# Queries and keys split once at full height and placed by DMA; the keys' low part kept once, its score product on 64 rows

## The chip, the cores and the metric

The kernel runs on one core of a Trainium2 chip. The metric is the device time of one execution in microseconds (us), less is better. The chip holds inputs and outputs in HBM, works in SBUF (128 partitions) and accumulates matrix products in PSUM. The engines are TensorE (PE in the profile; its weight loads are PEld), VectorE (DVE), ScalarE (ACT), GpSimd (POOL) and SyncE (SP), which here issues the DMAs.

## The reference, cut to what matters

One decoder layer over 1024 tokens of width 1024: a layer norm, then mixing, then a feed-forward part, then a gated embedding, each with a residual and a layer norm. The change is in the mixing, which has 8 attention heads of 64 features beside four pooling groups:

```
proj = x @ w_in[i]
q, k, v, u = jnp.split(proj, [ATTN_WIDTH, 2 * ATTN_WIDTH, 3 * ATTN_WIDTH], axis=-1)
...
z = jnp.einsum("bhqd,bhkd->bhqk", q_blk.astype(jnp.float32), kf) * scale
mask = k_pos[None, :] < q_pos[:, None]
log_not = jnp.where(mask, jax.nn.log_sigmoid(-z), 0.0)
suffix = lax.cumsum(log_not, axis=3, reverse=True) - log_not
weights = jnp.where(mask, jnp.exp(jax.nn.log_sigmoid(z) + suffix), 0.0)
return jnp.einsum("bhqk,bhkd->bhqd", weights, vf)
```

The attention is strictly causal, and instead of a softmax it breaks a stick: each weight is a sigmoid times the product of the complements that lie between.

## The kernel before, in words

All products are float32 made of parts: a number is split into a high part that TensorE's one-pass type (fp32r) holds, and the rest, the low part. `split` (L63) does it with a copy on ScalarE (L65) and a subtraction on VectorE (L66). A full product is three passes (`mm3`, L68 to L71): high by high, and the two mixed ones.

**Stages.** First the layer norm of all eight token blocks with the values' projection (to about 98 us). Then the attention stage (about 98 to 375 us). Then the output projection, the feed-forward part and the gate; the change doesn't touch these.

**The attention stage.** Work goes over tiles of one head and one block of 128 queries: four pairs of heads (`pr`), two heads in a pair (`j`), eight blocks (`t`), 64 tiles. `weigh` (L380) makes the scores of a tile against all keys up to its block, in chunks of 512 (`CH`): two products into one PSUM bank (L396, L397), two sigmoids on ScalarE (L398, L399), a reverse scan on VectorE (L400), a product on GpSimd (L403). `turn` transposes the weights (L126) and splits them; `gather` (every second tile, L429) multiplies them by the values.

TensorE's order is written out by hand: `weigh` runs three tiles (`AHEAD`) before `turn` and `gather`. Between them a stream called `fill` hands out steps of three products each: the projections of queries and keys of the pairs, then those of the pooling groups. `fill.until` makes sure that a pair's key chunk is projected before its first tile is weighed. The other engines' order, SP's too, is laid out by the framework's scheduler; semaphores and slots are assigned by it. Tiles come from tagged pools; tag `K` has 14 slots of 128x1024 float32.

**Queries and keys.** `proj_chunk` projects 128 columns, the two heads of a pair, for 512 tokens: head 0 comes out on partitions 0 to 63, head 1 on 64 to 127 (`rows[0]`, `rows[1]`). A head's 64 features are half of the array's 128 rows, so the kernel lays two parts of a query one over the other: in `qs[j]` the high part lies in the head's own half, the low part in the other. `kh[j]` holds the head's high keys in both halves. One product on 128 rows, `qs` by `kh` (L396), so gives high by high and low by high at once. The third part, high by low, is a second product on 128 rows: `kl[j]` holds the low keys in the head's own half and zeros, set by a memset (L268), in the other (L397).

`q_out` and `k_out` evacuate a chunk head by head: for each of the two heads a copy on 64 partitions (L259, L272) and a subtraction on 64 partitions (L260, L273). The low queries are written straight to the other half by VectorE; the high keys go to the other half by one DMA on SP's queue per head (L274).

Of the kernel before, what the change touches and what calls it, by code (L numbers as in the profile page):

```python
# [8 lines left out]
F32 = mybir.dt.float32  # L9
F32R = mybir.dt.float32r  # L10
AF = mybir.ActivationFunctionType
ALU = mybir.AluOpType
# [4 lines left out]
P = 128  # L17
S = 1024
# [3 lines left out]
CH = 512  # L22
# [12 lines left out]
def hymba_layer(ctx: ExitStack, tc: tile.TileContext, x, p, emb_g, emb_b, w_in, attn_g, w_pool,  # L35
                pool_scale, w_out, ln1_g, ln1_b, w_up, w_down, ln2_g, ln2_b, w_ple, w_gate,
                ln3_g, ln3_b, out):
    nc = tc.nc
    V, A, G, T = nc.vector, nc.scalar, nc.gpsimd, nc.tensor
    x, out, p = x[0], out[0], p[0, 0]  # L40
# [11 lines left out]
    def slot(tag, name, dt=F32):  # L52
        return sb.tile([P, 1024], dt, name=name, tag=tag, bufs=BUFS[tag])
# [5 lines left out]
    def bank(tag, name="bk"):  # L59
        return pspool.tile([P, CH], F32, name=name, tag=tag, bufs=2)  # L60


    def split(src, h, l, eng=None):  # L63

        A.copy(out=h, in_=src)  # L65
        (eng or V).tensor_tensor(out=l, in0=src, in1=h.bitcast(F32), op=ALU.subtract)  # L66
# [156 lines left out]
    rows = [slice(0, HD), slice(HD, P)]  # L223
# [10 lines left out]
    def proj_chunk(c0, c, evacuate):  # L234

        fetch(c0)
        wh, wl = loaded[c0]
        pq = bank("b0", "pq")
        for k in range(NK):
            mm3(pq, wh[:, k, :], wl[:, k, :], x_ap(xh, k, c), x_ap(xl, k, c),  # L240
                k == 0, k == NK - 1)
            if k == 1 and blocks.index(c0) + 1 < len(blocks):
                fetch(blocks[blocks.index(c0) + 1])
            if k == NK - 1:
                evacuate(slice(c * CH, (c + 1) * CH), pq)
            yield True

    def queries_keys(pr):

        t = {}

        def q_out(cs, pq):
            if "qs" not in t:
                t["qs"] = [slot("K", "qs", F32R) for _ in range(2)]
            for j in range(2):
                r, r2, qs = rows[j], rows[1 - j], t["qs"][j]
                A.copy(out=qs[r, cs], in_=pq[r])  # L259
                V.tensor_tensor(out=qs[r2, cs], in0=pq[r], in1=qs.bitcast(F32)[r, cs],  # L260
                                op=ALU.subtract)

        def k_out(cs, pq):
            if "kl" not in t:
                t["kl"] = [slot("K", "kl", F32R) for _ in range(2)]
                t["kh"] = [slot("K", "kh", F32R) for _ in range(2)]
                for j in range(2):
                    G.memset(t["kl"][j].bitcast(F32)[rows[1 - j], :], 0.0)  # L268
            for j in range(2):
                r, kh = rows[j], t["kh"][j]  # L270
                hf = kh.bitcast(F32)
                A.copy(out=kh[r, cs], in_=pq[r])  # L272
                V.tensor_tensor(out=t["kl"][j][r, cs], in0=pq[r], in1=hf[r, cs], op=ALU.subtract)  # L273
                nc.sync.dma_start(out=hf[rows[1 - j], cs], in_=hf[r, cs])  # L274

        for c in range(2):
            fill.add(proj_chunk(pr * P, c, q_out))
            fill.add(proj_chunk(512 + pr * P, c, k_out), (pr, c))
        return t

    def head_parts(t, j):
        return t["qs"][j], t["kh"][j], t["kl"][j]


    pspill = dram.tile([NT, P, D], F32, name="pspill")
# [30 lines left out]
    embedded = {}  # L316
    pw, pt = [], []
    heads = {pr: queries_keys(pr) for pr in range(4)}
    def leave0(i):
        load(xspill[i], xn[i])  # L320
# [48 lines left out]
    def head_values(pr, j):  # L369
        vs, h = slot("VS", "vs", F32R), 2 * pr + j  # L370
        load(vs.bitcast(F32).rearrange("p (t d) -> p t d", d=P),
             vspill[:, :, h * P:(h + 1) * P].rearrange("t p d -> p t d"))
        return vs.rearrange("p (t d) -> p t d", d=P)
# [6 lines left out]
    def weigh(k):  # L380

        if k.t == 0:
            k.vs = head_values(k.pr, k.j)
        else:
            k.vs = tiles[tiles.index(k) - 1].vs
        t, n = k.t, k.n
        qs, kh, kl = head_parts(heads[k.pr], k.j)
        if n <= CH:
            ra = slot("ra", "ra")
            rr, aa = ra[:, 0:CH], ra[:, CH:S]  # L390
        else:
            rr, aa = slot("ra", "rr"), slot("ra", "aa")
        for c in range(0, n, CH):
            e = min(n, c + CH)
            z = bank("b2", "z")[:, 0:e - c]
            T.matmul(z, lhsT=qs[:, t * P:(t + 1) * P], rhs=kh[:, c:e], start=True, stop=False)  # L396
            T.matmul(z, lhsT=qs[:, t * P:(t + 1) * P], rhs=kl[:, c:e], start=False, stop=True)  # L397
            A.activation(out=rr[:, c:e], in_=z, func=AF.Sigmoid, scale=-0.125)  # L398
            A.activation(out=aa[:, c:e], in_=z, func=AF.Sigmoid, scale=0.125)  # L399
        V.tensor_tensor_scan(out=rr[:, 0:n][:, ::-1], data0=rr[:, 0:n][:, ::-1],  # L400
                             data1=diag[:, S - n:S][:, ::-1], initial=0.0,
                             op0=ALU.mult, op1=ALU.add)
        G.tensor_tensor(out=aa[:, 0:n - 1], in0=aa[:, 0:n - 1], in1=rr[:, 1:n], op=ALU.mult)  # L403
        G.memset(aa[:, n - 1:n], 0.0)
        k.aa = aa
# [116 lines left out]
    with tc.manual_schedule(engines={mybir.EngineType.PE}):  # L522
        for n in range(-AHEAD, len(tiles)):
            if n >= 0:
                k = tiles[n]
                turn(k)
            if n + AHEAD < len(tiles):
                ahead = tiles[min(n + AHEAD + 1, len(tiles) - 1)]
                if ahead.j == 0 and ahead.t % 4 == 0:
                    fill.until((ahead.pr, ahead.t // 4))  # L530
                weigh(tiles[n + AHEAD])
            fill.rate = RATES[0] if n < 48 else RATES[1]
            if n < 0:
                fill.run(3)
            else:
                fill.share(k.n / P + 1.5)
                if k.t % 2:
                    gather(k)
                for f, *args in later.pop(n, ()):
                    f(*args)  # L540
                if k.j == 1 and k.t == NT - 1:
                    rms_square(k.pr)
                    later.setdefault(n + 2, []).append((rms_stats, k.pr))
                    later.setdefault(n + 8, []).append((rms_apply, k.pr, 0))
                    later.setdefault(n + 10, []).append((rms_apply, k.pr, 1))
        fill.run(4)
        rms_stats(3)
        fill.finish()
        rms_apply(3, 0)
        rms_apply(3, 1)  # L550
# [219 lines left out]
    for r0 in range(0, NT, 3):  # L770
# [4 lines left out]
        for n, k in enumerate(korder):  # L775
# [4 lines left out]
            for i in tiles:  # L780
                ts = slice(i * P, (i + 1) * P)
                for c in range(2):
                    cs = slice(c * CH, (c + 1) * CH)
# [17 lines left out]
        for i in tiles:  # L801
            for c in range(2):
                cs = slice(c * CH, (c + 1) * CH)
                V.scalar_tensor_tensor(out=xr[i][:, cs], in0=xr[i][:, cs], scalar=ALPHA,
                                       in1=acc[i, c], op0=ALU.mult, op1=ALU.add)
# [10 lines left out]
    with tc.manual_schedule(engines={ET.PE, ET.DVE, ET.Activation, ET.Pool}):  # L816

        stats = {}
        for i in (6, 7):
            for c in range(2):  # L820
                cs = slice(c * CH, (c + 1) * CH)
                V.scalar_tensor_tensor(out=xr[i][:, cs], in0=xr[i][:, cs], scalar=ALPHA,
                                       in1=acc[i, c], op0=ALU.mult, op1=ALU.add)
# [404 lines left out]
```

## Time and profile before

| what | value |
|---|---|
| median of 3 runs | 1255.14 us (1253.67 to 1256.07) |
| the profiled execution's own time | 1257.93 us |
| its span, from the first to the last instruction | 1256.2 us |
| mean granted clock of TensorE | 0.974 |
| PE, DVE, ACT, POOL busy | 1171.2, 942.5, 558.9, 523.4 us |

The profile is that of one execution. Busy times are sums over the whole span and over stages that have different limits. The ends of matmuls are modelled, and they overlap, so TensorE's busy time is not its time at its peak. A granted clock of 1 is 2.4 GHz.

### The profile page before, as it was taken

How to read it: one execution, taken by the hardware profiler on the slowest of the kernel's cores; microseconds unless marked ns; L12 is line 12 of the kernel's file. 1: busy time of each engine (PE TensorE's matmuls, PEld its weight loads, DVE VectorE, ACT ScalarE, POOL GpSimd, SP SyncE). 2: the span in 40 equal slices, each digit the busy share in tenths (PEclk: the TensorE clock that was granted, in tenths of full speed). 3: DMA queues.
4: the chain of work that ended last, by engine and by line, in shares of the span. 5: the costliest groups of instructions: out<-in, count | busy, mean ns of one | idle time of the engine just before them, and what ended most of it. 6: DMA issues, size and time to landing. Idle time of an engine off the chain costs nothing.

```text
span 1256.2 us, 15453 instructions
## 1 busy us (share of the span) xinstructions
PE 1171.2 (93%) x5496; PEld 965.3 (77%) x5496; DVE 942.5 (75%) x1177; ACT 558.9 (44%) x948; POOL 523.4 (42%) x360
## 2 busy tenths in 40 slices
PE   7999998899988998699899999999999999998997
PEld 5877777787877875488688888878888888886876
DVE  6745878686865779777577677778878888876998
ACT  4325756576654243445444545555432334421111
POOL 3212443354651353333434234247644556473432
PEclk9999999899998999899899999999999999998999
DMA  9824111121226364378777887899655665432121
GB/s 338 292 111 134 32 53 59 43 59 44 81 89 222 131 219 134 100 254 264 261 262 260 270 269 245 268 406 379 219 168 200 210 218 182 154 122 80 68 84 67
DMA packets 123580, 221.48 MB, mean 176 GB/s; under 512 B 9456, under 2 KB 64240, under 8 KB 123504
## 3 DMA queue, kind: packets, MB, share of 16 engines
q1 hardware_dynamic: 123504, 220.50, 51.8%
q8 instruction: 43, 0.70, 0.2%
q14 instruction: 33, 0.27, 0.1%
HBM read 148.12 MB, written 70.25 MB: 174 GB/s over the span
## 4 chain that ended last, share of the span: by engine, by line
PE 62%; DVE 15%; DMA 7%; issue 5%; POOL 5%; ACT 5%; SPq 1%; DVEq 0%; POOLq 0%; ACTq 0%
PE pd L69 7%; PE pd L70 7%; PE pd L71 7%; PE pu L71 5%; PE pu L70 5%; PE pu L69 5%; PE pq L69 3%; PE tp L126 3%; PE pq L70 2%; PE pq L71 2%; PE o L429 2%; DVE rr L400 2%; POOL rs L103 2%; DVE xres L113 2%; DMA tspill<-draw 1%
## 5 line engine op out<-in xcount | busy, mean ns | idle before, releaser
L574 POOL TENSOR_TENSOR draw<-draw 128x512 f32<-128x512 f32 x64 | 101.8, 1590 | 185.6 <-DMA draw<-in_w_down_dram 183.0
L922 DVE TENSOR_TENSOR xres<-xres,pd 128x512 f32<-128x512 f32 x208 | 137.1, 681 | 46.8 <-PE pd L71 46.2
L574 POOL TENSOR_TENSOR dop<-draw,dop 128x1024 fp32r<-128x1024 f32 (+1 forms) x48 | 112.8, 2369 | 125.8 <-ACT dop L899 112.3
L899 ACT CAST dop<-draw 128x1024 fp32r<-128x1024 f32 (+1 forms) x96 | 81.0, 906 | 137.9 <-PE pd L71 51.1
L69 PE MATMUL pd<-dop 128*128 128x512 f32 x320 | 125.4, 392 | 0.9 <-DVE xres L922 0.8
L70 PE MATMUL pd<-dop 128*128 128x512 f32 x320 | 125.1, 391 | 1.0 <-POOL dop L574 1.0
L71 PE MATMUL pd<-dop 128*128 128x512 f32 x320 | 124.8, 390 | 0.0
L574 DVE TENSOR_TENSOR dop<-draw,dop 128x1024 fp32r<-128x1024 f32 (+1 forms) x48 | 84.2, 1754 | 4.4 <-ACT dop L899 4.4
L103 POOL TENSOR_TENSOR rs<-var,mhalf 128x1 f32<-128x1 f32 x32 | 44.0, 1376 | 104.4 <-DVE var L101 104.3
L740 ACT COPY hid<-pu 128x512 f32<-128x512 f32 x48 | 28.2, 588 | 125.1 <-PE pu L71 74.5
L69 PE MATMUL pq<-xh,wh 128*128 128x512 f32 x192 | 78.4, 408 | 0.8 <-DVE ul L66 0.8
L400 DVE TENSOR_TENSOR_SCAN rr<-rr,diag 128x640 f32<-128x640 f32 (+3 forms) x32 | 70.6, 2205 | 10.7 <-ACT rr L398 10.3
L403 POOL TENSOR_TENSOR aa<-aa,rr 128x639 f32<-128x639 f32 (+3 forms) x32 | 57.8, 1806 | 48.6 <-DVE rr L400 48.6
L71 PE MATMUL pq<-xh,wl 128*128 128x512 f32 x192 | 77.1, 401 | 0.0
L70 PE MATMUL pq<-xl,wh 128*128 128x512 f32 x192 | 76.8, 400 | 0.0
L69 PEld LDWEIGHTS pd<-dop 128*128 128x128 f32 x320 | 60.3, 189 | 14.6 <-DVE xres L922 1.2
L70 PEld LDWEIGHTS pd<-dop 128*128 128x128 f32 x320 | 60.3, 189 | 14.0 <-POOL dop L574 1.7
L71 PEld LDWEIGHTS pd<-dop 128*128 128x128 f32 x320 | 60.3, 189 | 12.5
L574 DVE TENSOR_TENSOR hid<-pu,hid 128x512 f32<-128x512 f32 x48 | 33.0, 688 | 44.4 <-PE pu L71 37.7
L66 DVE TENSOR_TENSOR atl<-tp,ath 128x512 fp32r<-128x512 f32 (+2 forms) x96 | 50.9, 547 | 17.4 <-ACT ath L65 16.7
L65 ACT CAST wh<-wraw 128x1024 fp32r<-128x1024 f32 x36 | 38.0, 1056 | 47.1 <-PE acc L70 25.4
L70 PE MATMUL acc<-wl,mix 128*128 128x512 f32 x128 | 51.7, 404 | 4.6 <-POOL wl L66 4.2
(241 smaller groups left out, 3360.7 us busy)
## 6 DMA issues: line engine op xcount, KB each, us to landing
hspill<-hid SPq DMA_DIRECT2D x48, 512.0 KB, 5.2
draw<-hspill SPq DMA_DIRECT2D x48, 512.0 KB, 6.1
uraw<-in_w_up_dram SPq DMA_DIRECT2D x32, 512.0 KB, 5.8
draw<-in_w_down_dram SPq DMA_DIRECT2D x32, 512.0 KB, 4.7
tspill<-draw SPq DMA_DIRECT2D x64, 256.0 KB, 4.4
wraw<-in_w_out_dram SPq DMA_DIRECT2D x24, 512.0 KB, 3.6
draw<-in_w_down_dram SPq DMA_DIRECT2D x48, 256.0 KB, 5.2
wraw<-in_w_in_dram SPq DMA_DIRECT2D x16, 512.0 KB, 4.7
```

What stands on the lines that cost most here:

```text
L65: A.copy(out=h, in_=src)
L66: (eng or V).tensor_tensor(out=l, in0=src, in1=h.bitcast(F32), op=ALU.subtract)
L69: T.matmul(ps, lhsT=lh, rhs=rh, start=start, stop=False, **kw)
L70: T.matmul(ps, lhsT=lh, rhs=rl, start=False, stop=False, **kw)
L71: T.matmul(ps, lhsT=ll, rhs=rh, start=False, stop=stop, **kw)
L103: G.tensor_tensor(out=rs, in0=var, in1=mhalf[:, 0:1], op=ALU.pow)
L126: T.transpose(tp[:, j * P:(j + 1) * P], src[:, (k0 + j) * P:(k0 + j + 1) * P], ident)
L400: V.tensor_tensor_scan(out=rr[:, 0:n][:, ::-1], data0=rr[:, 0:n][:, ::-1], data1=diag[:, S - n:S][:, ::-1], initial=0.0, op0=ALU.mult, op1 ...
L403: G.tensor_tensor(out=aa[:, 0:n - 1], in0=aa[:, 0:n - 1], in1=rr[:, 1:n], op=ALU.mult)
L574: eng.tensor_tensor(out=o, in0=i0, in1=i1, op=op)
L899: A.copy(out=h, in_=raw)
L922: V.tensor_tensor(out=xres[i][:, cs], in0=xres[i][:, cs], in1=src, op=ALU.add)
```

## The change

`q_out` splits a chunk for both heads at once, on 128 partitions, into a staging slot (`qp`); four DMAs then place the parts in `qs`, two for each head. `k_out` does the same: the high part goes into a staging slot (`kp`), and four DMAs place each head's high keys in both halves of its `kh`; the low part goes straight into one tile `kl` for both heads, each in its own half. No half of `kl` is zeroed. The second score product reads only the head's own 64 rows of `qs` and `kl`.

```diff
         t = {}
+
+        def place(dst, src, j):
+            nc.sync.dma_start(out=dst, in_=src[rows[j]])
 
         def q_out(cs, pq):
             if "qs" not in t:
                 t["qs"] = [slot("K", "qs", F32R) for _ in range(2)]
+            both = slot("K", "qp", F32R)
+            h, l = both[:, 0:CH], both[:, CH:S]
+            split(pq, h, l)
             for j in range(2):
-                r, r2, qs = rows[j], rows[1 - j], t["qs"][j]
-                A.copy(out=qs[r, cs], in_=pq[r])
-                V.tensor_tensor(out=qs[r2, cs], in0=pq[r], in1=qs.bitcast(F32)[r, cs],
-                                op=ALU.subtract)
+                qs = t["qs"][j].bitcast(F32)
+                place(qs[rows[j], cs], h.bitcast(F32), j)
+                place(qs[rows[1 - j], cs], l.bitcast(F32), j)
 
         def k_out(cs, pq):
             if "kl" not in t:
-                t["kl"] = [slot("K", "kl", F32R) for _ in range(2)]
+                t["kl"] = slot("K", "kl", F32R)
                 t["kh"] = [slot("K", "kh", F32R) for _ in range(2)]
-                for j in range(2):
-                    G.memset(t["kl"][j].bitcast(F32)[rows[1 - j], :], 0.0)
+            h = slot("K", "kp", F32R)[:, 0:CH]
+            split(pq, h, t["kl"][:, cs])
             for j in range(2):
-                r, kh = rows[j], t["kh"][j]
-                hf = kh.bitcast(F32)
-                A.copy(out=kh[r, cs], in_=pq[r])
-                V.tensor_tensor(out=t["kl"][j][r, cs], in0=pq[r], in1=hf[r, cs], op=ALU.subtract)
-                nc.sync.dma_start(out=hf[rows[1 - j], cs], in_=hf[r, cs])
+                kh = t["kh"][j].bitcast(F32)
+                for r in rows:
+                    place(kh[r, cs], h.bitcast(F32), j)
...
     def head_parts(t, j):
-        return t["qs"][j], t["kh"][j], t["kl"][j]
+        return t["qs"][j], t["kh"][j], t["kl"]
...
             T.matmul(z, lhsT=qs[:, t * P:(t + 1) * P], rhs=kh[:, c:e], start=True, stop=False)
-            T.matmul(z, lhsT=qs[:, t * P:(t + 1) * P], rhs=kl[:, c:e], start=False, stop=True)
+            r = rows[k.j]
+            T.matmul(z, lhsT=qs[r, t * P:(t + 1) * P], rhs=kl[r, c:e], start=False, stop=True)
```

## Rows read from the trace of the kernel before

**Rows 1.** The page's engine totals: busy us, share of the span, instructions.
```profile
PE 1171.2 (93%) x5496; PEld 965.3 (77%) x5496; DVE 942.5 (75%) x1177; ACT 558.9 (44%) x948; POOL 523.4 (42%) x360
```

**Rows 2.** Windows view of the attention stage, 100 to 375 us.
```profile
core 0: us, PE busy (x) PEld busy (x) DVE busy (x) ACT busy (x) POOL busy (x), PEclk, DMA share, GB/s
100.00:375.00 275.00, 254.25 (x1420) 216.08 (x1418) 206.80 (x258) 171.49 (x393) 128.18 (x149) 0.96 0.22 63
```

**Rows 3.** Chain of waits, 98 to 380 us: shares, then pieces (start, us).
```profile
by line: PE pq L69 10.2%; PE pq L70 9.8%; PE pq L71 9.7%; PE o L429 9.4%; PE tp L126 8.0%; DVE rr L400 8.0%; issue 6.6%; DVE atl L66 3.9%; PE z L396 3.7%; PE z L397 3.3%; ACT rr L398 3.0%; DVE wl L66 2.9%; ACT aa L399 2.6%; PE pm L447 2.3%;
...
113.23 2.25 DMA kh<-kh
...
131.17 0.68 DVE qs L260
...
287.52 0.60 DVE kl L273
```

**Rows 4.** Groups by line, 0 to 560 us: count, busy us, mean ns, idle before.
```profile
L396 PE MATMUL z<-kh,qs 128*128 128x512 f32 (+2 forms) x96 | 40.1, 418 | 6.1 <-ACT ra L399 3.9 <-DMA kh<-kh 2.1
L397 PE MATMUL z<-kl,qs 128*128 128x512 f32 (+2 forms) x96 | 33.8, 356 | 0.0
L260 DVE TENSOR_TENSOR qs<-pq,qs 64x512 fp32r<-64x512 f32 x16 | 11.0, 689 | 7.6 <-ACT qs L259 7.3
L273 DVE TENSOR_TENSOR kl<-pq,kh 64x512 fp32r<-64x512 f32 x16 | 10.9, 684 | 2.1 <-ACT kh L272 1.9
L259 ACT CAST qs<-pq 64x512 fp32r<-64x512 f32 x16 | 9.3, 583 | 13.1 <-PE pq L71 6.6 <-DVE qs L260 6.5
L272 ACT CAST kh<-pq 64x512 fp32r<-64x512 f32 x16 | 9.3, 582 | 7.0 <-DVE kl L273 6.5 <-PE pq L71 0.3
L268 POOL MEMSET kl<- 64x1024 f32 x8 | 7.6, 948 | 22.4 <-PE pe L70 22.0
L66 DVE TENSOR_TENSOR ul<-pq,uh 128x512 fp32r<-128x512 f32 x8 | 5.4, 678 | 3.0 <-ACT uh L65 3.0
L65 ACT CAST uh<-pq 128x512 fp32r<-128x512 f32 x8 | 4.8, 602 | 4.0 <-PE pq L71 4.0
```

**Rows 5.** Source view of L274: issue time on SP in ns, and landing.
```profile
L274 SPq DMA_DIRECT2D kh<-kh x16: 461/467/523, 94.0 to 288.8; - x16
...
DMA to landing us min/median/max: 2.2/2.3/3.7
```

**Rows 6.** Timeline of SP, 165 to 172 us, and two copies on ScalarE.
```profile
166.99 0.47 SPq L274 DMA_DIRECT2D kh<-kh  x1
167.77 0.37 SPq L74 DMA_DIRECT2D wraw<-in_w_in_dram  x1
169.31 0.47 SPq L274 DMA_DIRECT2D kh<-kh  x1
171.52 0.37 SPq L74 DMA_DIRECT2D vs<-vspill  x1
...
166.39 0.57 ACT L272 CAST kh<-pq 64x512 fp32r<-64x512 f32 x1
...
256.33 0.58 ACT L272 CAST kh<-pq 64x512 fp32r<-64x512 f32 x1 [0.30 <-PE pq L71]
```

**Rows 7.** Timeline of TensorE: first score products on those two key chunks.
```profile
172.75 0.48 PE L396 MATMUL z<-kh,qs 128*128 128x512 f32 x1
...
284.31 0.30 PE L396 MATMUL z<-kh,qs 128*128 128x128 f32 x1
```

**Rows 8.** Timeline of TensorE, 112.2 to 113.3 us: start, us.
```profile
112.25 0.39 PE L396 MATMUL z<-kh,qs 128*128 128x512 f32 x1
112.48 0.39 PE L397 MATMUL z<-kl,qs 128*128 128x512 f32 x1
112.71 0.38 PE L126 MATMUL tp<-ident,ra 128*128 128x128 f32 x2
112.84 0.48 PE L396 MATMUL z<-kh,qs 128*128 128x512 f32 x1
```

**Rows 9.** Timeline of weight loads, from 115.58 us, under products in flight.
```profile
115.69 0.19 PEld L397 LDWEIGHTS z<-kl,qs 128*128 128x128 f32 x1
115.80 0.19 PEld L69 LDWEIGHTS pq<-xh,wh 128*128 128x128 f32 x1
```

**Rows 10.** Windows view, 240 to 250 us; columns as in rows 2.
```profile
240.00:250.00 10.00, 10.00 (x41) 9.02 (x40) 4.29 (x4) 3.22 (x8) 4.82 (x5) 0.52 0.00 1
```

## The prediction

> **What bounds the kernel now.** I read the page's engine totals first, to see which engine could be the limit at all: TensorE is busy 93% of the span and VectorE 75% [rows 1]. That is an average over stages, and the change touches one of them, the attention stage. So I asked for that stretch alone, 100 to 375 us: TensorE 254.25 of 275 us, VectorE 206.80, ScalarE 171.49, GpSimd 128.18, DMA share 0.22 [rows 2]. The reader is to see that TensorE is nearest to full, that VectorE is not free either, and that the DMA engines have room.
>
> Next the chain of waits over the stretch, since a busy share doesn't say who waits for whom. TensorE holds 10.2 + 9.8 + 9.7 + 9.4 + 8.0 + 3.7 + 3.3 + 2.3 = 56.4% of it by the lines named, VectorE's scan 8.0%, its low parts (L66) 3.9% [rows 3]. So the stage is a weave: more than half of the time the end is set by TensorE's stream, the rest by short steps on VectorE and ScalarE that TensorE then waits for. The instructions that the change rewrites stand on this chain themselves: 14 pieces on L259, L260 and L273, from 131.17 to 287.52 us, sum 9.08 us; and one transfer of a key half, 2.25 us [rows 3].
>
> **The split, removed and added.** Each pair of heads has two chunks, so there are 8 query and 8 key evacuations. Before, each takes two copies and two subtractions on 64 partitions: 16 + 16 copies of 0.58 us, 9.3 + 9.3 us on ScalarE; 16 + 16 subtractions of 0.69 us, 11.0 + 10.9 us on VectorE [rows 4]. After, each takes one copy and one subtraction on 128 partitions. The pool's values go through just that pair already: 0.602 and 0.678 us at 128x512 [rows 4]; height costs nothing. So ScalarE sheds 18.6 - 16 x 0.60 = 9.0 us and VectorE 21.9 - 16 x 0.68 = 11.0 us. GpSimd sheds 8 memsets, 7.6 us [rows 4]; it is under half busy in the stage [rows 2], so I take nothing for it.
>
> Of this only what stands on the chain moves the end. Copy, subtraction, copy, subtraction run one behind the other (ScalarE sat idle 6.5 us before L259 and 6.5 us before L272 until the subtraction had ended [rows 4]); half of that series is left. Half of 9.08 is **-4.5 us**. Bounds: nothing, if other work on VectorE fills the place, and -11.0 us, if all that VectorE sheds came off the end.
>
> **The moves.** After, a query chunk and a key chunk are placed by four DMAs each: 64 in all where there were 16. An issue on SP takes 0.467 us, and one lands 2.3 us after it [rows 5]. SP thus gets 48 x 0.467 = 22.4 us more in a queue that carried one or two DMAs in ten microseconds here (between 165 and 172 us: four issues [rows 6]). Behind a move that waits for its copy or its subtraction stand, on SP, the next weight block and the next head's values, and ScalarE's weight cast waits for the former. Latency: before, copy, then one DMA: 0.58 + 2.3 us. After, the first head's key chunk needs two: 0.60 + 0.47 + 2.3, the last of four 0.60 + 3 x 0.467 + 2.3 = 4.3 us. What covers it is the lead of the projection: the copy for pair 1's second chunk is at 166.39 and its first score product at 172.75, 6.4 us [rows 6, 7]; pair 3's first chunk is copied at 256.33 and used at 284.31 [rows 6, 7]. Only the transfer at 113.23 had no cover [rows 3]; it ends one issue later, **+0.5 us** (bounds 0 and 1.4, all four). The query parts are projected a whole key chunk (24 products of some 0.23 us, 5.5 us) earlier. Of the 14 slots the long-lived tiles of a pair take 5 instead of 6; two short-lived staging slots come in. Nothing for either.
>
> **The second product on 64 rows.** Its streamed columns are unchanged, so by itself it costs what it did; nothing gained, since the next product needs all rows. But all 96 pairs of score products now alternate in height: into 64 rows and out again, 192 changes. No row shows a product of that height: the array part reads 128*128 everywhere, L396 and L397 included [rows 4]. What rows do show is how much equal heights overlap. Products of 512 columns start at 112.25 and 112.48, 0.23 apart, and each lasts 0.39 [rows 8]: 0.16 us of each runs under the next. The next weights also load under the product in flight, 0.11 apart [rows 9]. Lower bound of a change: 0, overlap as before. Upper bound: the product ends, then the weights load, 0.16 + 0.11 = 0.27 us. I take 0.16, an estimate: the product in flight is let run to its end before the other height starts, while the weights are fetched ahead as now; it lies between the ends, and uses only an overlap that rows show to exist. That makes 192 x 0.16 = 30.7 us of TensorE. TensorE holds 56.4% of the chain, and a delay counts where it does: **+17.3 us**. Bounds for that share: 27% (the score products' own 7.0% of 282 us is 19.7 us of their 40.1 + 33.8), 8.2 us; and all of it, 30.7 us.
>
> The Trainium skill, TensorEngine Tiling (Array Packing), section Tiling Modes, Key Properties, says that changing the tiling mode, as against the tile, drains the engine; no run here shows it yet. It gives no time; by it the sum is the one above, and without it the first rival's. The Trainium skill, TensorE: Matmul & The Clock Gate, Part 3, says that a weight load overlaps a product in flight only when their row groups differ. Here the measurement differs: [rows 9] has loads 0.11 us apart beneath products on the same 128 rows. By the page the load would wait in the forecast too, which is the second rival's sum.
>
> **The sum.** -4.5 + 0.5 + 17.3 = +13.3 us. It stands against the profiled execution: 1257.93 us, 1.73 beyond its span of 1256.2. The median of the runs shown is 2.79 lower, 1255.14; so the time forecast is 1255.1 + 13.3 = **1268.4 us**. Its own range, by the two shares: +4.2 to +26.7, 1259 to 1282.
>
> **Rivals.** *Height is free*: products of both heights follow each other 0.23 us apart. Then -4.5 + 0.5 = -4.0, 1251.1 us; at best -11, 1244. For it: kinds of TensorE work change without a gap now, transposes into score products at 112.71 and 112.84 [rows 8]. Against it: those all use the full array. It decides if a change costs under 4.0 / (192 x 0.564) = 0.037 us. *Weights wait too*: 0.27 us, 51.8 us of TensorE, x 0.564 = 29.2; less 4.0, +25.2, 1280 us; more if TensorE then holds the whole chain (+47.8, 1303). Against it: loads run ahead today [rows 9]. *The moves gate*: heights free, but SP's order puts a move behind a wait, and one place without cover pays a full 3 x 0.467 + 2.3 = 3.7 us: -4.0 + 3.7 = -0.3, 1254.8 us. For it: the 2.25 us on the chain and 4 times the DMAs [rows 3, 5]. Against: leads of 6 to 28 us, and SP nearly empty [rows 6, 7].
>
> **Chances.** Forecast 0.50: the change of height is the one new thing on the engine that is nearest to full, and a quarter of the price taken is enough to outweigh the gain. Height free 0.27; weights wait too 0.12; moves gate 0.11. About 0.2% is what a measurement of this kernel can tell from no change, 2.5 us. Faster: most of the first rival and a little of the last, 0.27. Within 0.2%: most of the last rival, the edge of the others, 0.10. Slower: forecast and second rival, 0.63. The range, 1247 to 1290, leaves out the best end of the free case and the worst of the third, under 2 in 10.
>
> **What the changed profile would show.** Right: L397's successors (and L397 itself) start some 0.39 us after the product before them instead of 0.23, with the array part 64*128; the stretch of attention longer by 10 to 20 us, all others unchanged; 16 copies and 16 subtractions at 128x512, 64 moves on SP, and the copy-subtraction pieces on the chain halved. Wrong: starts still 0.23 apart (first rival), loads that begin only at the product's end (second), TensorE waiting for moves (third). The forecast is wrong above all if the change of height is cheap, or if the copies' time on the chain was worth more than half; and if the gaps let the granted clock fall, as between 240 and 250 us (0.52) [rows 10], it is too low.

## The result, and the profile after

The changed kernel takes 1274.25 us (median of 4 runs, 1271.42 to 1280.91), against 1254.41 for the kernel before beside it: a ratio of 1.0157, 95% interval 1.0132 to 1.0182, some 19.7 us more. It is slower, as forecast; the forecast was 13.3 us more.

The execution profiled is the slowest of the four (1280.91 us), at a mean granted clock of 0.966 where the others had 0.971 to 0.976; its totals stand a little high for that. Its page's engine totals, to be held against [rows 1]:

```profile
PE 1210.9 (95%) x5496; PEld 975.1 (76%) x5496; DVE 922.1 (72%) x1161; ACT 552.7 (43%) x932; POOL 507.8 (40%) x352
```

VectorE and ScalarE have 16 instructions less each and GpSimd 8, as the split promised; TensorE is busy 39.7 us more with the same number of products, a part of it by the lower clock. Two of the four groups of the new split, at 128x512, against [rows 4]:

```profile
L65 ACT CAST qp<-pq 128x512 fp32r<-128x512 f32 x8 | 4.7, 592 | 9.3 <-PE pq L71 9.3
...
L66 DVE TENSOR_TENSOR kl<-pq,kp 128x512 fp32r<-128x512 f32 x8 | 5.5, 682 | 4.1 <-ACT kp L65 4.1
```

With their counterparts that is 11.0 us of VectorE where it was 21.9, and 9.4 of ScalarE where it was 18.6. The attention stage in the windows view, columns as in [rows 2], and the chain of waits from 98 to 400 us, against [rows 3]:

```profile
100.00:375.00 275.00, 269.16 (x1295) 205.46 (x1294) 178.15 (x221) 154.97 (x353) 106.40 (x136) 0.93 0.29 76
```

```profile
by line: PE pq L69 16.9%; PE pq L70 13.0%; PE pq L71 12.9%; PE o L434 11.9%; PE z L402 11.5%; PE tp L126 10.4%; PE z L400 7.9%; DMA qs<-qp 1.9%; PE pm L452 1.9%; DVE rr L405 1.4%; DVE atl L66 1.0%; issue 0.9%; POOL aa L408 0.9%; PE pb L465 
...
111.64 5.79 DMA qs<-qp
```

Three things are to be seen. TensorE is now full in the stage (269.16 of 275 us) and got through 1295 products in it instead of 1420. It holds 86.4% of the chain by the lines named, where it held 56.4%; VectorE's scan fell from 8.0% to 1.4%. And a new wait stands on the chain: 5.79 us for query moves, where 2.25 us was for a key half.

Now the products themselves. The timeline of TensorE and of its weight loads around one pair of score products, against [rows 8, 9]:

```profile
114.28 0.39 PE L71 MATMUL pq<-xh,wl 128*128 128x512 f32 x1
114.50 0.39 PE L400 MATMUL z<-kh,qs 128*128 128x512 f32 x1
114.82 0.50 PE L402 MATMUL z<-kl,qs 64*128 64x512 f32 x1
115.25 0.44 PE L126 MATMUL tp<-ident,ra 128*128 128x128 f32 x2
117.47 0.76 PE L400 MATMUL z<-kh,qs 128*128 128x512 f32 x1 [1.78 <-DMA qs<-qp]
```

```profile
114.28 0.19 PEld L400 LDWEIGHTS z<-kh,qs 128*128 128x128 f32 x1
114.82 0.18 PEld L402 LDWEIGHTS z<-kl,qs 64*128 64x128 f32 x1 [0.35 <-issue]
115.25 0.20 PEld L126 LDWEIGHTS tp<-ident,ra 128*128 128x128 f32 x2 [0.24 <-issue]
```

L400 follows L71 at the old distance. L402, on 64 of 128 rows, doesn't: its weight load, which used to begin 0.00 to 0.11 us behind the start of the product before it, begins 0.32 us behind, when that product is all but over (it ends at 114.89). Its own end comes 115.32 - 114.89 = 0.43 us after the last one's, where the same pair was 0.23 us apart in [rows 8]. The 0.32 is the shortest of its kind; the median of 41 such pairs of 512 columns at full clock is 0.41. What stays the same is the end: in all 83 changes into 64 rows at full clock, whatever the columns, the load begins 0.07 us before the modelled end of the product before it (at 512 columns it was 0.40 us before it in the kernel before). The way back costs as much: behind L402, whatever its columns, a product of 512 columns ended 0.43 us later (median of 70 cases; before, 0.24). So a change of height costs 0.20 us at 512 columns, 0.19 at 256 and 384, 0.14 at 128: about the length of the load itself (0.18 us in the row above), which is no longer hidden. Weighted by the counts of L402's forms (48, 16, 16, 16) that is 17.9 us into the low products and some 19 us out of them: about 37 us of TensorE for 192 changes.

The moves, last. First SP's timeline before the wait; then, by the tile view, the landing of the values' loads (104 to 107 us), of the moves of high parts (109.5 to 111.5 us), and of all query moves, against [rows 5]; then three windows, columns as in [rows 2]:

```profile
104.99 2.21 SPq L74 DMA_DIRECT2D vs<-vspill  x3
109.83 1.11 SPq L256 DMA_DIRECT2D qs<-qp  x2
111.04 0.53 SPq L74 DMA_DIRECT2D wraw<-in_w_in_dram  x1
111.64 2.50 SPq L256 DMA_DIRECT2D qs<-qp  x2
```

```profile
DMA to landing us min/median/max: 4.0/5.8/7.5
...
DMA to landing us min/median/max: 4.7/4.7/4.8
...
DMA to landing us min/median/max: 2.2/2.4/5.8
```

```profile
110.00:113.00 3.00, 3.00 (x15) 2.44 (x14) 1.81 (x3) 0.15 (x1) 0.00 (x0) 1.00 1.13 261
113.00:116.00 3.00, 2.69 (x12) 1.62 (x10) 1.12 (x1) 2.12 (x4) 0.00 (x0) 1.00 1.10 235
119.00:122.00 3.00, 3.00 (x8) 2.28 (x9) 1.49 (x1) 1.41 (x4) 0.26 (x3) 0.50 0.61 178
```

The two moves of high parts went out, then a 512 KB weight block, then the moves of low parts. Most moves land in 2.4 us; these took 4.2 to 5.8, while the DMA engines were full (share 1.13 and 1.10; a packet counts whole where it starts, so a share can pass 1). The weight block is not alone in this: the high parts went out ahead of it and took 4.7 us too, while two of three 512 KB loads of values, issued from 104.99 us on, were still landing. TensorE stood for 1.78 us, and ran at half clock behind it (0.50 from 119 to 122 us).

### The profile page after: what moved, and what is told of

It reads as the page before. It is cut to its first block, busy times and chain, and to the rows that moved or that the text cites. A ratio compares the mean times of both kernels' runs of the same rounds, so it can differ in the third digit from the quotient of the medians.

```text
span 1279.1 us, 15507 instructions
## 1 busy us (share of the span) xinstructions
PE 1210.9 (95%) x5496; PEld 975.1 (76%) x5496; DVE 922.1 (72%) x1161; ACT 552.7 (43%) x932; POOL 507.8 (40%) x352
## 4 chain that ended last, share of the span: by engine, by line
PE 73%; DVE 10%; DMA 6%; POOL 5%; issue 4%; ACT 2%; SPq 0%; DVEq 0%; POOLq 0%; ACTq 0%
PE pd L69 7%; PE pd L70 7%; PE pd L71 7%; PE pu L69 7%; PE pu L71 7%; PE pu L70 7%; PE pq L69 4%; PE pq L70 3%; PE pq L71 3%; PE tp L126 3%; PE o L434 3%; PE z L402 3%; PE z L400 2%; POOL rs L103 2%; DVE xres L113 2%
## 5 line engine op out<-in xcount | busy, mean ns | idle before, releaser
L71 PE MATMUL pd<-dop 128*128 128x512 f32 x320 | 125.0, 391 | 0.0
L69 PE MATMUL pq<-xh,wh 128*128 128x512 f32 x192 | 85.7, 447 | 1.6 <-DVE vst L66 1.6
L405 DVE TENSOR_TENSOR_SCAN rr<-rr,diag 128x640 f32<-128x640 f32 (+3 forms) x32 | 65.5, 2047 | 23.2 <-ACT rr L403 20.8
L71 PE MATMUL pq<-xh,wl 128*128 128x512 f32 x192 | 78.4, 408 | 0.0
L71 PEld LDWEIGHTS pd<-dop 128*128 128x128 f32 x320 | 60.5, 189 | 12.6
```

Of the source, the lines that this page charges most:

```text
L69: T.matmul(ps, lhsT=lh, rhs=rh, start=start, stop=False, **kw)
L71: T.matmul(ps, lhsT=ll, rhs=rh, start=False, stop=stop, **kw)
```

## The experiments

Two theories after the result. The first: the changes of height are the cost, and TensorE as the new bound eats what the split saves. The rival: the 48 added moves are the cost. All ratios are to the kernel before, run beside the experiment; a ratio of 1.001 is 1.25 us.

**One part alone, and the other.** In the first run the kernel before gets the 64-row product and nothing else; in the second the changed kernel gets its 128-row product back, with the low keys in two tiles with zeroed halves.

```diff
# e1_rows64_only, from the kernel before
-            T.matmul(z, lhsT=qs[:, t * P:(t + 1) * P], rhs=kl[:, c:e], start=False, stop=True)
+            r = rows[k.j]
+            T.matmul(z, lhsT=qs[r, t * P:(t + 1) * P], rhs=kl[r, c:e], start=False, stop=True)
# e3_rows128_moves, from the changed kernel
-                t["kl"] = slot("K", "kl", F32R)
+                t["kl"] = [slot("K", "kl", F32R) for _ in range(2)]
...
+                for j in range(2):
+                    G.memset(t["kl"][j].bitcast(F32)[rows[1 - j], :], 0.0)
             h = slot("K", "kp", F32R)[:, 0:CH]
-            split(pq, h, t["kl"][:, cs])
+            A.copy(out=h, in_=pq)
+            for j in range(2):
+                r = rows[j]
+                V.tensor_tensor(out=t["kl"][j][r, cs], in0=pq[r], in1=h.bitcast(F32)[r],
+                                op=ALU.subtract)
...
-            r = rows[k.j]
-            T.matmul(z, lhsT=qs[r, t * P:(t + 1) * P], rhs=kl[r, c:e], start=False, stop=True)
+            T.matmul(z, lhsT=qs[:, t * P:(t + 1) * P], rhs=kl[:, c:e], start=False, stop=True)
```

> The kernel before with one edit: the second score product reads only the head's own 64 rows; the split, the zeroed halves and the moves stay as before. If changes of height on TensorE are the cost (theory), all of it is here and none of what the full-height split saves: 20 to 28 us slower than before, and every product behind a change starts some 0.2 us late. If the 48 added moves are the cost (rival), it runs as before, within 3 us.

> The changed kernel with the second score product on 128 rows again: full-height copies, the queries' full-height subtraction, all 64 moves, but the keys' low part in two tiles with zeroed halves, by two subtractions of 64 partitions. Theory: without the changes of height the split's gain shows, 2 to 7 us faster than before. Rival (the moves): 15 to 20 us slower, like the changed kernel.

Measured: e1 1.0138 (1.0121 to 1.0155), 17.3 us slower; e3 1.0039 (1.0022 to 1.0056), 4.9 us slower. The height alone gives nearly the whole loss: the first theory, a little under its forecast. But e3 is no 2 to 7 us faster: the moves cost something of their own, and the forecast gain doesn't show. The attention stage of e1 in the windows view:

```profile
100.00:375.00 275.00, 268.44 (x1314) 206.05 (x1314) 191.21 (x239) 165.62 (x376) 115.14 (x144) 0.95 0.19 56
```

TensorE is full without a single added move. In e3 the chain of waits shows what is left of the rival: two pieces, 10.76 us, the first of pair 0 and the second of pair 1, where [rows 3] had one of 2.25:

```profile
111.27 7.18 DMA qs<-qp
159.79 3.58 DMA qs<-qp
```

**Fewer changes of height.** The changed kernel, with both 128-row products of a two-chunk tile made before both 64-row ones:

```diff
+        zs = {}
         for c in range(0, n, CH):
...
-            z = bank("b2", "z")[:, 0:e - c]
+            z = zs[c] = bank("b2", "z")[:, 0:e - c]
             T.matmul(z, lhsT=qs[:, t * P:(t + 1) * P], rhs=kh[:, c:e], start=True, stop=False)
-            r = rows[k.j]
+        for c in range(0, n, CH):
+            e = min(n, c + CH)
+            z, r = zs[c], rows[k.j]
```

> The changed kernel, but a tile with two chunks makes both products on 128 rows first and then both on 64 rows: 128 changes of height instead of 192. Theory: a third of the price goes, so some 7 to 9 us less than the changed kernel, 10 to 14 us slower than before; less is won if the sigmoids that now wait for the second product matter. Rival (the moves): as the changed kernel, within 3 us.

Measured: 1.0119 (1.0104 to 1.0134), 14.9 us slower, 4.8 less than the changed kernel: the right way, about half of the size forecast. Its timeline tells height from change:

```profile
152.00 0.60 PE L401 MATMUL z<-kh,qs 128*128 128x512 f32 x2
152.53 0.61 PE L405 MATMUL z<-kl,qs 64*128 64x512 f32 x2
153.07 0.50 PE L69 MATMUL pq<-xh,wh 128*128 128x512 f32 x1
```

The row L405 x2 is a product of 512 and one of 256 columns, both on 64 rows. Together they last 0.61 us, as long as the two on 128 rows ahead of them (0.60). A low product behind a low product is free; only the change costs.

**Half of the changes.** The kernel before, with the low product on 64 rows for one head of each pair; 96 changes in either run:

```diff
# e2_rows64_head0; e9_rows64_head1 has slice(HD, P) if k.j else slice(0, P)
-            T.matmul(z, lhsT=qs[:, t * P:(t + 1) * P], rhs=kl[:, c:e], start=False, stop=True)
+            r = slice(0, HD) if k.j == 0 else slice(0, P)
+            T.matmul(z, lhsT=qs[r, t * P:(t + 1) * P], rhs=kl[r, c:e], start=False, stop=True)
```

> As the run before, but only for the first head of each pair: 96 changes of height instead of 192. Theory: half of what e1_rows64_only adds, 10 to 14 us slower than before. If a first few changes already cost all (TensorE becomes the bound at once, or the clock falls), much more than half. Rival (the moves): as before, within 3 us.

> As e2_rows64_head0, but for the second head of each pair: again 96 changes of height. If each change costs TensorE some 0.2 us and the time follows the delay, half of e1's 17 us: 7 to 12 us slower, and e2's 18 us was its clock's doing (0.963 to 0.969, where e1 had 0.971 to 0.976). Rival (half of the changes already makes TensorE the bound, and the rest is free): 15 to 19 us again.

Measured: e2 1.0143 (1.0125 to 1.0161), 17.9 us slower, as much as both heads together; e9 1.0033 (1.0011 to 1.0055), 4.1 us, less than forecast. So the time as measured doesn't follow the number of changes. Nor is one half of the rows dearer than the other: the low product of 512 columns ends 0.43 us behind the high one in e2 and in e9 (medians of 21 and 24 pairs at full clock). Windows of one head each: the third head before, and in e2; then the fourth head before, and in e9.

```profile
159.29:190.23 30.94, 28.79 (x170) 24.70 (x168) 21.25 (x29) 19.74 (x46) 14.80 (x19) 0.94 0.17 44
190.23:220.08 29.85, 27.40 (x164) 23.29 (x164) 25.62 (x32) 19.69 (x46) 10.91 (x18) 1.00 0.21 62
```

```profile
159.60:198.63 39.03, 38.52 (x170) 29.30 (x168) 21.29 (x30) 20.44 (x46) 15.57 (x20) 0.78 0.13 35
```

```profile
192.93:224.07 31.14, 31.10 (x164) 23.88 (x163) 25.59 (x32) 19.91 (x46) 10.95 (x18) 1.00 0.20 59
```

In e9 the fourth head's TensorE is busy 3.7 us longer, and the head takes 1.3 us longer: TensorE had 2.45 us idle there and used them. In e2 the third head takes 8.1 us longer; its granted clock is 0.78 where it was 0.94, so 8.6 us of full speed are lost in it instead of 1.9, and this is 6.7 of the 8.1. That is one execution, but e2's four runs all have a mean clock of 0.963 to 0.969, e1's 0.971 to 0.976. An estimate of what this is worth: over the runs of the kernel before, 0.001 of mean clock went with 0.8 to 1.4 us, and e2's mean of 0.967 is 0.0066 below theirs, 5 to 9 us. Without them e2 stands at 9 to 13 us; with e9's 4.1 that makes 13 to 17, where both heads together gave 17.3. So the changes of both runs add up to about the whole, the first heads' share being the larger. Why the first heads' changes lower the clock more than both heads' together is open.

**Where the moves cost.** e3 with pair 0 split and placed as before; e3 with the keys' moves alone; e3 with the queries' alone; and e3 with the projections' weight blocks loaded from ScalarE's DMA queue.

```diff
# e5_pair0_direct: q_first and k_first are q_out and k_out of the kernel before
-            fill.add(proj_chunk(pr * P, c, q_out))
-            fill.add(proj_chunk(512 + pr * P, c, k_out), (pr, c))
+            fill.add(proj_chunk(pr * P, c, q_out if pr else q_first))
+            fill.add(proj_chunk(512 + pr * P, c, k_out if pr else k_first), (pr, c))
# e6_keys_only: e3 with q_out of the kernel before; e7_queries_only: with its k_out
# e8_loads_other_queue, in load_split; col_block passes queue=nc.scalar
-        load(raw.rearrange(*shape[:1], **shape[1]) if shape else raw, src)
+        (queue or nc.sync).dma_start(out=raw.rearrange(*shape[:1], **shape[1]) if shape else raw,
+                                     in_=src)
```

> As e3_rows128_moves (1259.7 us, 4.9 above before), but pair 0, whose second chunk has no lead, is split and placed as before; pairs 1 to 3 by moves. Theory: in e3 the chain waits 7.18 us for the query moves of pair 0, which were issued right behind a 512 KB weight load, where before it waits 2.25 us; without this wait 4 to 6 us less than e3, 1254 to 1256 us. Rival (the moves cost in all pairs, by SP's queue or by DMA traffic): a quarter less at most, 1258 to 1260 us.

> As e3_rows128_moves, but the queries as before: only the keys are copied at full height and moved. Theory: the waits on the chain of e3 are for query moves, so this one is as before or a little faster, 1251 to 1255 us. Rival (any move costs): half of e3's loss, some 1257 us.

> As e3_rows128_moves, but the keys as before: only the queries are split at full height and moved. Theory: it has the waits of e3 for query moves, 3 to 7 us slower than before, 1257 to 1262 us. Rival (any move costs): half of e3's loss, some 1257 us; rival (the keys' moves are the cost): as before.

> As e3_rows128_moves, but the projections' weight blocks are loaded from ScalarE's DMA queue instead of SP's, so that no move stands behind a 512 KB load. Theory (the move waits for the load ahead of it in its queue): the query moves land in 2.2 to 3.5 us instead of up to 7.2, the waits of 7.18 and 3.58 us on the chain go to 3 us or less, 1251 to 1255 us. Rival (moves and loads share the DMA engines, whatever the queue): the slow landings stay, 1258 to 1260 us.

Measured: e5 0.9985 (0.9971 to 0.9999), 1.9 us faster than before and 6.8 less than e3: pair 0 was it. In its chain of waits the piece of 7.18 us is gone, and so is that of 3.58, though pair 1 is still placed by moves; what is left is this:

```profile
112.68 2.25 DMA kh<-kh
128.26 2.26 DMA qs<-qp
```

The two traces place the difference. e3's first score product starts at 101.99 us and e5's at 99.12; its first head takes 31.5 us and e5's 29.3; the second and third heads, with the piece of 3.58 us, take the same in both (30.1 and 29.6).

e6 is 1.0028 (1.0011 to 1.0045), 3.5 us slower: a miss, the keys' moves of pair 0 have a price too (its chain waits 2.40 us for them, and its first score product starts at 100.74 instead of 99.67). e7 is 1.0012 (0.9995 to 1.0030), 1.5 us: below the forecast, and not told from no change, though its chain holds waits of 7.19 and 3.60 us as e3's does. So the length of a wait on the chain is not its price. e8 is 1.0055 (1.0034 to 1.0075): the theory of the queue's order fell, as far as the weight block goes. Its moves and its load went out on two queues (timelines of SP and ScalarE), and the moves landed about as late (tile view of the queries, 109 to 112.2 us):

```profile
109.02 2.92 SPq L257 DMA_DIRECT2D qs<-qp  x4
...
110.24 0.38 ACTq L78 DMA_DIRECT2D wraw<-in_w_in_dram  x1
```

```profile
DMA to landing us min/median/max: 5.2/6.0/6.8
```

The values' loads were still ahead of these moves on SP. A later place of the same trace has no load on SP since 145.38 us: four key moves of one chunk, with a weight block going out on ScalarE's queue between the second and the third (timelines; then the tile view of the high keys, 170 to 171.2 and 171.2 to 172.4 us):

```profile
170.06 2.39 SPq L257 DMA_DIRECT2D kh<-kp  x4
...
170.84 0.37 ACTq L78 DMA_DIRECT2D wraw<-in_w_in_dram  x1
```

```profile
DMA to landing us min/median/max: 2.3/2.5/2.7
...
DMA to landing us min/median/max: 5.2/5.2/5.3
```

The two moves ahead of the block landed in 2.3 and 2.7 us, the two behind it in 5.3 and 5.2. So a load in another queue holds a move up, which leaves the DMA engines as the place where the two meet.

**The rest of the sum.** e10: 128 rows, keys as before, queries moved in pairs 1 to 3. e11: the changed kernel with pair 0 as before (its low keys in the one tile).

> Second product on 128 rows, keys as before, queries split at full height and moved in pairs 1 to 3 only. Theory: the wait of pair 0 is gone and half of the split's gain is left, 1 to 4 us faster than before. Rival (the moves' gain needs both, or is noise): as before, within 1.5 us.

> The changed kernel (64 rows, one low-part tile, moves), but pair 0 placed as before. If the late moves of pair 0 are a cost of their own beside the changes of height, 4 to 7 us less than the changed kernel, 13 to 16 us slower than before. Rival (TensorE, now the bound, works off something else meanwhile): as the changed kernel, 19 to 20 us slower.

Measured: e10 0.9997 (0.9975 to 1.0020), no change that can be told. e11 1.0086 (1.0056 to 1.0116), 10.8 us slower than before, 8.9 less than the changed kernel: more than forecast. TensorE as the bound doesn't hide the late moves; it stands while they are awaited.

The kernel that beats both is e5: full-height copies, moves where the projection runs ahead, 128 rows. By 1.9 us, with an interval that ends at 0.9999, this is little.

## Why the prediction was right, and where its sizes were off

**The mechanism was right in the main.** The prediction said that the change of height on TensorE decides, that the product in flight is let run to its end before the other height starts, and that the split's saving is smaller than this. e1 shows the first: the height alone is 17.3 us. The loads that begin at the end of the product before show the second. But the prediction also had the weights fetched ahead as now, and they aren't: it had named loads that begin only at the product's end as the sign of its second rival. The Trainium skill, TensorEngine Tiling (Array Packing), Key Properties, says that changing the tiling mode drains the engine; the trace agrees, at 0.20 us a change. e4 adds that staying in the mode is free, for two products on the same 64 rows.

**The term of 17.3 us came out as 17.3 us by two errors that cancel.** The price of a change was taken as 0.16 us and is 0.20, between the forecast and the second rival's 0.27: a load of 0.18 us comes out of hiding, and the lost overlap of 0.16 is not added to it. So 37 us instead of 30.7. The share of it that reaches the end was taken as TensorE's share of the chain, 56.4%; e1's 17.3 of 37 is 47%. A share of the chain was a fair exchange rate, no more: e2 and e9 give 17.9 and 4.1 us for 18 us of delay each.

**The step that was mis-sized is the moves:** +0.5 us, bounds 0 and 1.4. They cost some 7 to 9 us: the changed kernel against e11, 8.9 (their intervals leave some 5 us either way, and e11's runs also had the higher clock, 0.973 to 0.978); e3 against e5, 6.8 (some 3 either way). The prediction had one place without cover, the key transfer at 113.23 us. The runs show two more, both in pair 0. One lies before the first score product: it starts at 100.47 to 101.99 us in the six kept traces that move pair 0, and at 98.96 to 100.00 in the seven that write it directly. The other is the query parts, which the prediction let pass with "nothing for either" because they are projected 5.5 us earlier, and a landing was priced at the row's 2.3 us. From the copy at 109.20 us to the product that had to wait (from 115.69) there were 6.5 us; of them the copy took 0.60, the subtraction began at 110.93, behind a weight split on VectorE, and the moves of the low parts, issued from 111.64 on, took up to 5.8 us to land beside 512 KB loads. The 2.3 us of [rows 5] is a median: of its sixteen moves the four that went out 1.2 to 2.2 us behind a weight block took 3.4 to 3.7 us, the row's maximum. How the price divides is open: e6 puts 3.5 us on the keys' moves and e7 1.5 on the queries', against the waits on the chain. Of the rival in which the moves gate, the mechanism was right, then, at one pair; but it came on top of the forecast, not in its place.

**The split's -4.5 us** lies between what two pairs of runs show, each with three pairs of heads of four: e11 against e1, -6.5 us; e5 against before, -1.9. The two are not the same saving: e11 is rid of all memsets, e5 keeps them and subtracts the keys head by head. Their intervals leave some 4 us either way in the first, so a gain is shown, with TensorE as the bound too, and its size isn't.

Summed from the runs: 17.3 for the height, -6.5 for the split, 8.9 for the moves of pair 0, 19.7 us. The three are differences of one chain of runs, so that they add up is no check. The first rival, height is free, fell with e1; *weights wait too* was right about the load, and its 25.2 us too high. The 19.7 us lie about midway between that and the forecast's 13.3.

What the prediction asked to see: products 0.39 us after the one before in place of 0.23 (seen: at 512 columns ends 0.43 us apart, starts 0.41), array part 64*128 (seen), the copies at 128x512, their pieces on the chain halved (more than that: the chain's 195 longest pieces hold two of them, 0.53 and 0.68 us), the stretch of attention longer by 10 to 20 us (26: its first head begins at 100.79 instead of 99.67 us and its last score products at 377.63 instead of 350.48). Of its signs of being wrong three stood beside these: the late loads, TensorE waiting for a move, and a lower granted clock, 0.93 in the stage where it was 0.96, in the executions profiled.

## What to carry to other kernels

A product that uses half of the rows is no cheaper than one padded with zeros, and if its neighbours use all rows it costs 0.2 us on the way in and again on the way out: pad it, or put such products side by side. A move that replaces a direct write needs a lead measured at the busiest moment it can meet; the usual landing time is that of DMA engines with little else to carry, and another queue does not get round a load. So write directly where the lead is short; where it is long, moves gained little or nothing on 128 rows (1.9 us in e5, none that can be told in e10). And before shortening work on engines that share a chain with TensorE, see that TensorE doesn't get longer by the same edit: here 192 changes of height took more than the split gave.

## What the runs showed that was not expected

The granted clock of the changed kernel stood at its lower level, 1.2 GHz, for several microseconds behind the wait of 1.78 us, and again from the time of 16 products of two columns on (the row below; timeline of TensorE, then windows):

```profile
184.86 2.54 PE L452 MATMUL pm<-hm,sq 128*128 128x2 f32 x16
```

```profile
188.00:191.00 3.00, 3.00 (x7) 1.58 (x7) 0.70 (x2) 2.08 (x5) 2.70 (x1) 0.50 0.00 0
191.00:194.00 3.00, 3.00 (x11) 2.36 (x9) 1.78 (x2) 0.62 (x2) 2.80 (x3) 0.50 0.00 0
```

The narrow products alone don't bring it about. The kernel before has such a stretch around the same work [rows 10], but its clock was down before they began at 241.94 us, behind a stretch in which TensorE was busy 1.86 of 4 us; and behind those that began at 305.79 us it stayed full (three windows of the kernel before):

```profile
236.00:240.00 4.00, 1.86 (x8) 1.23 (x7) 2.48 (x5) 3.71 (x8) 0.72 (x2) 0.92 0.47 133
240.00:242.00 2.00, 2.00 (x9) 1.71 (x8) 1.81 (x1) 0.00 (x0) 0.61 (x3) 0.50 0.01 4
308.00:312.00 4.00, 4.00 (x23) 3.38 (x22) 2.52 (x3) 3.90 (x9) 3.27 (x4) 1.00 0.00 0
```

What decides it is open. The mean clock differs from execution to execution, and much of the spread of one kernel goes with it: e8 ran in 1252.04 us at a mean clock of 0.978 and in 1266.92 at 0.969.
